# A factored one-hot for the first key, products four apart in PSUM, and another share of the activations per block

## The chip, the core and the metric

One core of a Trainium2 chip. TensorE does matmuls from SBUF into PSUM, VectorE the elementwise work, ScalarE activations and the reading out of PSUM, GpSimd issues the gathers, and a queue on SyncE issues the other transfers. The metric is the device time of one execution in microseconds, lower is better.

## What is computed

One layer of an encoder on 512 tokens of width 1024. The first half (sparse attention beside a pooling mixer) is not touched here. The second half looks up experts by product keys:

```python
def peer_ffn(h, w_q, sub_keys, u, v):          # by blocks of 128 tokens
    q = (hx @ w_q).reshape(TOKEN_BLOCK, PEER_HEADS, 2, PEER_HALF)
    s = jnp.einsum('nhpd,hpkd->nhpk', q, sub_keys)
    top_s, top_i = lax.top_k(s, PEER_TOPK)
    ...
    expert = (i1 * N_KEYS + i2).reshape(TOKEN_BLOCK, PEER_HEADS * PEER_TOPK)
    gate = jax.nn.softmax(best_s, axis=-1)
    act = jax.nn.gelu(jnp.einsum('nd,ned->ne', hx, u[expert]), approximate=False)
    return jnp.einsum('ne,ned->nd', gate * act, v[expert])
```

Each token takes 128 pairs (8 heads, 16 each) of a first key `i1` and a second key `i2`, both 0 to 127, with a gate each; there are 128 x 128 experts.

## The kernel before

Three of the four blocks of 128 tokens (384 tokens) are done densely: the activation of every expert is computed for all of them, times a table of gates that is zero where an expert wasn't chosen. The last block gathers its experts' rows.

The stage around the change I call the **gates stage**. Three kinds of work are recorded side by side there:

- The dense activations, `dense_acts`: 128 chunks of 128 experts. A chunk loads 512 KB of `uT`, ScalarE rounds it (`uhe`, line 517), VectorE makes the rest (`ule`, line 518), TensorE does 24 matmuls of 384 columns (`pse`, lines 554 to 556), ScalarE takes the gelu (line 563). 59 chunks are done in and around this stage, and the other 69 in the last stage, beside the contraction with `v`. `act_until(n)` records activations until n eighths of a chunk are there.
- The product keys of the coming block (`pk.pairs`, `pk.halves`): top 16 by VectorE, softmax, keys written to `sel`.
- The gates, `gates(tb)`, for blocks 0, 1 and 2. The keys and gates of a block are transposed, so that a partition is one of the 128 pairs and a column a token. Then for every 8 tokens VectorE makes two one-hot tables, `one` of the first key (line 614) and `two` of the second (line 615), each 128 x (8 tokens x 128 keys) in 16 bits, and multiplies `one` with the gates, which are in two 16-bit parts (line 620, twice). For each token TensorE multiplies `two` (as weights) with the gated `one`, one matmul of 128 columns per part, both into one 128 x 128 piece of PSUM (`gm`, line 626): the token's table of gates. Four tokens fill one PSUM tile; ScalarE scales it into `st` (line 627), where 16 tokens lie side by side per expert, so it writes single 4-byte values 64 bytes apart. Every 16 tokens a transfer of 1 MB writes `st` out to `gd`.

A step of 4 tokens is one `yield` of `gates`; after each step the loop records some of the keys' work and calls `act_until`, so that the activations are spread evenly over the 96 steps. The order of recording is not the whole order: the scheduler of the tile layer moves instructions of an engine past one another where their inputs and buffers allow. Each engine then runs its own list in that order. After the third block the chunks that are left run (`act_until` twice), and then the last stage opens, whose buffers take the place of this stage's.

Of the kernel before, what the change touches and what calls it, by code (L numbers as in the profile page):

```python
# [40 lines left out]
LEAD = 10  # L41
# [24 lines left out]
def layer(ctx, tc, xT, cvec, w_ada, cols, consts, w_in, w_grp, w_up, w_out, w_pq, subk, u, uT, v, out):  # L66
    nc = tc.nc
    V, A, T, G = nc.vector, nc.scalar, nc.tensor, nc.gpsimd
# [18 lines left out]
    iota = con[:, K_IOTA:K_IOTA + P]  # L87
    blk = con[:, K_BLK:K_BLK + P]

    with ExitStack() as pre:  # L90
# [110 lines left out]
        with ExitStack() as mix:  # L201
# [33 lines left out]
            with tc.tile_pool(name="xp", bufs=1, reuse_waits="tile") as xp, tc.tile_pool(name="xq", bufs=1, reuse_waits="tile") as xq, \  # L235
# [4 lines left out]
                ps = pst.tile([P, S], F32, name="n1s")  # L240
                part = tmp.tile([P, S], F32, tag="nf", name="n1p")
# [11 lines left out]
                for d in range(DT):  # L253
# [5 lines left out]
                    if rs is None:  # L259
# [3 lines left out]
                                           op0=ALU.add, op1=ALU.mult)  # L263
# [30 lines left out]
            ps = linear("q0", hh, hl)  # L294
# [41 lines left out]
            for i in range(4):  # L336
# [9 lines left out]
                ps = nxt  # L346
# [45 lines left out]
            for g in range(1, 4):  # L392
                ps = linear(f"p{g}", hh, hl)
# [5 lines left out]
            for j in range(DT):  # L399
                ps = linear(f"gp{j}", hh, hl)  # L400
# [130 lines left out]
    def multiply(w, n, name):  # L531
        return multiplies([w], n, [name])[0]
# [35 lines left out]
    with ExitStack() as win:  # L568
        kp = win.enter_context(tc.tile_pool(name="kp", bufs=1, reuse_waits="tile"))
        kt = win.enter_context(tc.tile_pool(name="kt", bufs=1, reuse_waits="tile"))  # L570
        oh = win.enter_context(tc.tile_pool(name="oh", bufs=2, reuse_waits="tile"))
        plg = win.enter_context(tc.tile_pool(name="plg2", bufs=2, space=PSUM, reuse_waits="tile"))
        pgm = win.enter_context(tc.tile_pool(name="pgm", bufs=2, space=PSUM, reuse_waits="tile"))
        ptr = win.enter_context(tc.tile_pool(name="ptr2", bufs=1, space=PSUM, reuse_waits="tile"))
        irep = kp.tile([P, NEXP, 2], F16, name="irep")
        V.tensor_copy(irep, iota.unsqueeze(2).to_broadcast([P, NEXP, 2]))
        pq = kp.tile([P, NH, S], F32, name="pq")
        sk = kp.tile([P, NH, P], F32, name="sk")
        nc.sync.dma_start(out=sk, in_=subk)
        pk = ProductKeys(nc, kp, kt, plg, pq, sk)  # L580
        for h in range(0, NH, 2):
            two = [fetch(w_pq[i], f"pq{i}") for i in (h, h + 1)]
            if h:
                two = [multiply(w, S, f"pq{h}_{i}") for i, w in enumerate(two)]
            else:
                two = multiplies(two, S, ["pq0_0", "pq0_1"])
            for i in range(2):
                A.copy(pq[:, h + i, :], two[i])
            for tb in range(2):
                pk.halves(tb, h)  # L590

        def gates(tb):

            tr = ptr.tile([P, 4, P], F32, tag="tr", name=f"gtr{tb}")
            for i, x in enumerate(sel[tb]):
                T.transpose(tr[:, i, :], x, ident)

            keys = oh.tile([P, 2, P], F16, tag="keys", name=f"keys{tb}", bufs=1)
            part = oh.tile([P, 2, P], F16, tag="part", name=f"part{tb}", bufs=1)
            gs = oh.tile([P, P], F32, tag="gs", name=f"gs{tb}", bufs=1)  # L600
            A.copy(keys, tr[:, 0:2, :])
            A.activation(gs, tr[:, 2, :], AF.Copy, scale=2.0 ** SCALED)
            A.copy(part[:, 0, :], gs)
            V.tensor_tensor(part[:, 1, :], gs, part[:, 0, :], op=ALU.subtract)

            full = [P, 4, NEXP, 2]
            pairs = lambda x, t: x[:, t:t + 8].rearrange("p (q j) -> p q j", j=2).unsqueeze(2).to_broadcast(full)
            numbers = irep.unsqueeze(1).to_broadcast(full)
            for g in range(P // GT):
                st = oh.tile([P, NEXP, GT], F32, tag="st", name=f"st{tb}_{g}", bufs=STB)  # L610
                for t8 in range(0, GT, 8):
                    t = g * GT + t8
                    one, two = [oh.tile(full, F16, tag=f"on{i}", name=f"on{i}_{tb}_{t}") for i in range(2)]
                    V.tensor_tensor(one, numbers, pairs(keys[:, 0, :], t), op=ALU.is_equal)  # L614
                    V.tensor_tensor(two, numbers, pairs(keys[:, 1, :], t), op=ALU.is_equal)  # L615
                    gated = []
                    for i in range(2):
                        x = oh.tile(full, F16, tag=f"oa{i}", name=f"oa{i}_{tb}_{t}")
                        gated.append(x)
                        V.tensor_tensor(x, one, pairs(part[:, i, :], t), op=ALU.mult)  # L620
                    for t4 in range(0, 8, 4):
                        ps = pgm.tile([P, 4, P], F32, tag="gm", name=f"gm{tb}_{t + t4}")
                        for k in range(4):
                            q, j = (t4 + k) // 2, k % 2
                            for i in range(2):
                                T.matmul(ps[:, k, :], two[:, q, :, j], gated[i][:, q, :, j], start=(i == 0), stop=(i == 1))  # L626
                        A.activation(st[:, :, t8 + t4:t8 + t4 + 4].rearrange("p e t -> p t e"), ps, AF.Copy, scale=2.0 ** -SCALED)  # L627
                        yield
                nc.sync.dma_start(out=gd[tb * (P // GT) + g], in_=st)

        sel = {}

        def select(tb):
            sel[tb] = [kt.tile([P, P], F32, tag=f"sel{i}", name=f"sel{tb}_{i}", bufs=2) for i in range(3)]
            return pk.pairs(tb, *sel[tb])

        def coming(tb):
            yield from select(tb)
            if tb + 1 < TB:
# [12 lines left out]
        for _ in select(0):
            act_until(done + DT)
        act_until(LEAD * DT)
        steps = P // 4
        between = (KEPT + SPILL - LEAD - TRAIL) * DT
        for tb in range(DENSE):
            keys = coming(tb + 1)
            for n, _ in enumerate(gates(tb)):
                if n * KEYS[tb] // steps != (n + 1) * KEYS[tb] // steps:  # L660
                    next(keys, None)
                act_until(LEAD * DT + between * (tb * steps + n + 1) // (DENSE * steps))
            for _ in keys:
                pass
        hs = kt.tile([P, DT, P], F32, tag="pr", name="hs")
        V.tensor_tensor(hs, h2h[:, :, ND:].bitcast(F32), h2l[:, :, ND:].bitcast(F32), op=ALU.add)
        for j0 in range(0, DT, 4):
            ps = ptr.tile([P, 4, P], F32, tag="tr", name=f"hxp{j0}")
            for j in range(4):
                T.transpose(ps[:, j, :], hs[:, j0 + j, :], ident)  # L670
            A.copy(hx[:, j0 * P:(j0 + 4) * P].rearrange("p (j t) -> p j t", t=P), ps)
        act_until((KEPT + SPILL) * DT)
        act_until(10 ** 6)
        k1, k2, g3 = sel[DENSE]
        V.scalar_tensor_tensor(e3, k1, 128.0, k2, op0=ALU.mult, op1=ALU.add)
        V.tensor_copy(gate3, g3)
# [80 lines left out]
    with tc.manual_schedule(engines={mybir.EngineType.DVE, mybir.EngineType.PE, mybir.EngineType.Activation}):  # L757
# [6 lines left out]
        for c in range(NEXP):  # L764
            a = c + KEPT
# [205 lines left out]
```

## Time and profile before

| | us |
|---|---|
| median of 3 runs (1596.89 to 1604.06) | 1600.07 |
| the profiled execution | 1600.14 |
| its span, first to last instruction | 1598.3 |
| gates stage, first gates' work on VectorE to the last gates' matmul | about 478 to 726 |
| its blocks | 478 to 563, 563 to 650, 650 to 726 |

The profile is read first by its 40 slices, then by windows of the one stage, by who waited for whom, by the chain of work that ended last, and by groups of instructions of one shape. A duration in a group is from an instruction's start to its end; neighbours on an engine can overlap by a little, so what one costs its engine is read from the starts of a row of them.

### The profile page before, as it was taken

Reading aid. Unit: us, or ns where it says so; the run is one execution under the profiler, and the core shown is the slowest. Engines: PE = TensorE matmul, PEld = TensorE weight load, DVE = VectorE, ACT = ScalarE, POOL = GpSimd, SP = SyncE. Lnnn points to the kernel's source line nnn. Section 1 sums busy time; section 2 is a strip of 40 time slices with the busy share of each in tenths; the row PEclk is TensorE's granted clock in tenths of the full one; section 3 lists DMA queues with packets and bytes.
Section 4 is the critical chain, followed back from the end, with each engine's and each line's share of the span. In section 5 each row is a group of like instructions: output and inputs, shape, how many; then the busy total and the mean of one; then the engine's idle time right before and its main releaser. Section 6 shows DMA issues by size and latency. Waiting matters only on the chain.

```text
span 1598.3 us, 22373 instructions
## 1 busy us (share of the span) xinstructions
PE 1540.0 (96%) x7977; PEld 1311.7 (82%) x7977; DVE 1311.6 (82%) x2658; ACT 691.3 (43%) x993; POOL 326.1 (20%) x318
## 2 busy tenths in 40 slices
PE   5999999999999999999999999999999999999998
PEld 3678766786789888899778999999999999987776
DVE  7799776658999999995668888888888888887777
ACT  4543445534446675674333333333333333333332
POOL 0000000000000000001113444444544445442320
PEclk9999999999999999999999999999999999999999
DMA  8412654333235454669889999999999999987874
GB/s 309 165 66 86 214 186 121 117 148 119 66 119 195 163 190 173 229 234 322 301 288 340 322 364 332 339 360 316 361 336 337 355 318 363 339 289 261 273 274 171
DMA packets 155105, 393.91 MB, mean 246 GB/s; under 512 B 13041, under 2 KB 67953, under 8 KB 151922
## 3 DMA queue, kind: packets, MB, share of 16 engines
q1 hardware_dynamic: 118130, 258.25, 46.5%
q0 software_dynamic: 36864, 134.23, 23.8%
q8 instruction: 62, 1.02, 0.3%
q14 instruction: 49, 0.40, 0.1%
HBM read 358.75 MB, written 33.69 MB: 246 GB/s over the span
## 4 chain that ended last, share of the span: by engine, by line
PE 48%; DVE 10%; DMA 5%; ACT 1%; issue 1%; SPq 0%; ACTq 0%; DVEq 0%
PE acc L748 28%; PE pse L540 6%; PE pse L539 6%; PE pse L538 6%; DMA v<-v 5%; DVE oa L620 2%; DVE ule L518 2%; DVE on L614 1%; DVE on L615 1%; ACT vh L738 1%; DVE vl L740 1%; PE pse L556 1%; PE pse L555 1%; PE pse L554 1%; PE gm L626 0%
## 5 line engine op out<-in xcount | busy, mean ns | idle before, releaser
L689 POOL DMA_INDIRECT ur<-u,ei x128 | 158.0, 1234 | 638.7 <-ACT Wh L737 395.0
L748 PE MATMUL acc<-vh,Wh 128*128 128x512 f32 x768 | 240.3, 394 | 14.6 <-ACT vh L738 14.6
L748 PE MATMUL acc<-vl,Wh 128*128 128x512 f32 x768 | 241.2, 395 | 2.0 <-DVE vl L740 1.9
L748 PE MATMUL acc<-vh,Wl 128*128 128x512 f32 x768 | 240.1, 394 | 0.0
L740 DVE TENSOR_TENSOR vl<-v,vh 128x1024 fp32r<-128x1024 f32 x128 | 156.9, 1226 | 83.0 <-ACT vh L738 70.7
L697 POOL DMA_INDIRECT vr<-v,ei x128 | 165.2, 1291 | 232.7 <-DVE sacc L702 204.2
L540 PE MATMUL pse<-h2h,ule 128*128 128x384 f32 x552 | 185.1, 335 | 0.0
L539 PE MATMUL pse<-h2l,uhe 128*128 128x384 f32 x552 | 184.6, 334 | 0.0
L538 PE MATMUL pse<-h2h,uhe 128*128 128x384 f32 x552 | 184.4, 334 | 0.0
L737 ACT ACTIVATE Wh<-gelu 128x384 fp32r<-128x384 f32 x106 | 55.6, 525 | 290.1 <-PE acc L748 187.5
L748 PEld LDWEIGHTS acc<-vh,Wh 128*128 128x128 f32 x768 | 144.7, 190 | 41.6 <-ACT vh L738 16.7
L748 PEld LDWEIGHTS acc<-vl,Wh 128*128 128x128 f32 x768 | 145.7, 191 | 35.3 <-DVE vl L740 5.3
L748 PEld LDWEIGHTS acc<-vh,Wl 128*128 128x128 f32 x768 | 146.2, 190 | 30.9
L518 DVE TENSOR_TENSOR ule<-ue,uhe 128x1024 fp32r<-128x1024 f32 x128 | 155.9, 1218 | 19.0 <-ACT uhe L517 19.0
L554 PE MATMUL pse<-h2h,uhe 128*128 128x384 f32 x472 | 166.2, 352 | 1.0 <-ACT gelu L563 1.0
L556 PE MATMUL pse<-h2h,ule 128*128 128x384 f32 x472 | 161.1, 342 | 4.7 <-DVE ule L518 4.5
L702 DVE SCALAR_TENSOR_TENSOR sacc<-vr,wt,sacc 128x1024 f32<-128x1024 f32 x127 | 162.8, 1282 | 2.4
L555 PE MATMUL pse<-h2l,uhe 128*128 128x384 f32 x472 | 159.6, 338 | 0.0
L517 ACT ACTIVATE uhe<-ue 128x1024 fp32r<-128x1024 f32 x128 | 134.8, 1053 | 53.8 <-PE pse L555 36.0
L691 DVE SCALAR_TENSOR_TENSOR ur<-ur,hx 128x1024 f32<-128x1024 f32 x128 | 150.7, 1220 | 1.5 <-DMA ur<-u,ei 1.5
L738 ACT ACTIVATE vh<-v 128x1024 fp32r<-128x1024 f32 x128 | 135.7, 1060 | 36.0 <-DMA v<-v 35.7
L627 ACT ACTIVATE st<-gm 128x512 f32<-128x512 f32 x96 | 101.2, 1092 | 53.9 <-PE gm L626 49.6
(412 smaller groups left out, 2757.3 us busy)
## 6 DMA issues: line engine op xcount, KB each, us to landing
ue<-uT SPq DMA_DIRECT2D x128, 512.0 KB
v<-v SPq DMA_DIRECT2D x128, 512.0 KB
wada<-w_ada SPq DMA_DIRECT2D x48, 512.0 KB
gd<-st SPq DMA_DIRECT2D x24, 1024.0 KB
g<-gd SPq DMA_DIRECT2D x16, 1536.0 KB
ad<-gelu SPq DMA_DIRECT2D x22, 192.0 KB
wgp<-w_in SPq DMA_DIRECT2D x8, 512.0 KB
wga<-w_in SPq DMA_DIRECT2D x8, 512.0 KB
```

The costliest lines, as they stand in the source:

```text
L518: V.tensor_tensor(lo, src, hi.bitcast(F32), op=ALU.subtract)
L538: T.matmul(p, hi[:, k, :], h2h[:, k, :n], start=(k == 0), stop=False)
L539: T.matmul(p, hi[:, k, :], h2l[:, k, :n], start=False, stop=False)
L540: T.matmul(p, lo[:, k, :], h2h[:, k, :n], start=False, stop=(k == DT - 1))
L554: T.matmul(ps, hi[:, k, :], h2h[:, k, :ND], start=(k == 0), stop=False)
L555: T.matmul(ps, hi[:, k, :], h2l[:, k, :ND], start=False, stop=False)
L556: T.matmul(ps, lo[:, k, :], h2h[:, k, :ND], start=False, stop=(k == DT - 1))
L689: G.indirect_dma_start(out=ur, out_offset=None, in_=u, in_offset=bass.IndirectOffsetOnAxis(ap=ei3[:, k:k + 1], axis=0))
L697: G.indirect_dma_start(out=vr, out_offset=None, in_=v, in_offset=bass.IndirectOffsetOnAxis(ap=ei3[:, k:k + 1], axis=0))
L702: V.scalar_tensor_tensor(sacc, vr, wt[:, k:k + 1], sacc, op0=ALU.mult, op1=ALU.add)
L740: V.tensor_tensor(vl, vr, vh.bitcast(F32), op=ALU.subtract)
L748: T.matmul(acc[tb][i], x[:, t], y[:, i * 512:(i + 1) * 512], start=(c == 0 and n == 0), stop=(c == NEXP - 1 and n == 2))
```

## The change

The first key is split as 16 a + b, with a from 0 to 7 and b from 0 to 15. `low` is b, `keys[:, 0, :]` becomes 16 a (four small instructions a block). For every 32 tokens VectorE makes `rest`, the one-hot of b over 16 numbers (128 x 512), `ten`, the one-hot of a over 8 (128 x 256), and `gt`, `ten` times each part of the gates (twice 128 x 256). The gated table of 8 tokens is then a product of `gt` and `rest`, spread over 8 x 16 keys (128 x 1024, twice as before); `one` is gone.

The order of the axes in the gated table, in the PSUM tile and in the reading out is another: the PSUM tile is `[128, 128 keys, 4 tokens]`, so a matmul writes its 128 columns 16 bytes apart, and ScalarE reads the tile straight through and writes four tokens (16 bytes) at a time, 64 bytes apart.

`FILL` sets the share of the activations that is recorded by the end of each block: 0.36, 0.72 and 1.0, in place of a third each.

```diff
+tens = kp.tile([P, NEXP // KL, 8], F16, name="tens")
+V.tensor_copy(tens, iota.rearrange("p (a b) -> p a b", b=KL)[:, :, 0:1].to_broadcast([P, NEXP // KL, 8]))
...
+ki = oh.tile([P, P], I32, tag="ki", name=f"ki{tb}", bufs=1)
+V.tensor_copy(ki, keys[:, 0, :])
+V.tensor_scalar(ki, ki, KL - 1, None, op0=ALU.bitwise_and)
+V.tensor_copy(low, ki)
+V.tensor_tensor(keys[:, 0, :], keys[:, 0, :], low, op=ALU.subtract)
...
+                if g * GT % TG == 0:
+                    rest = oh.tile([P, TG // 2, KL, 2], F16, tag="rest", name=f"rest{tb}_{g}")
+                    V.tensor_tensor(rest, numbers(TG // 2, KL), pairs(low, t, TG).to_broadcast([P, TG // 2, KL, 2]), op=ALU.is_equal)
+                    ten = oh.tile([P, NG, NA, 8], F16, tag="ten", name=f"ten{tb}_{g}")
+                    V.tensor_tensor(ten, tens.unsqueeze(1).to_broadcast([P, NG, NA, 8]), eights(keys[:, 0, :], t), op=ALU.is_equal)
+                    for i in range(2):
+                        V.tensor_tensor(gt[i], ten, eights(part[:, i, :], t), op=ALU.mult)
...
-                    V.tensor_tensor(one, numbers, pairs(keys[:, 0, :], t), op=ALU.is_equal)
...
-                        V.tensor_tensor(x, one, pairs(part[:, i, :], t), op=ALU.mult)
+                        V.tensor_tensor(x, gt[i][:, n].rearrange("p a (q j) -> p a q j", j=2).unsqueeze(3).to_broadcast([P, NA, 4, KL, 2]),
+                                        rest[:, 4 * n:4 * n + 4].unsqueeze(1).to_broadcast([P, NA, 4, KL, 2]), op=ALU.mult)
...
-                        ps = pgm.tile([P, 4, P], F32, tag="gm", name=f"gm{tb}_{t + t4}")
+                        ps = pgm.tile([P, P, 4], F32, tag="gm", name=f"gm{tb}_{t + t4}")
...
-                                T.matmul(ps[:, k, :], two[:, q, :, j], gated[i][:, q, :, j], start=(i == 0), stop=(i == 1))
-                        A.activation(st[:, :, t8 + t4:t8 + t4 + 4].rearrange("p e t -> p t e"), ps, AF.Copy, scale=2.0 ** -SCALED)
+                                T.matmul(ps[:, :, k], two[:, q, :, j], gated[i][:, :, q, :, j], start=(i == 0), stop=(i == 1))
+                        A.activation(st[:, :, t8 + t4:t8 + t4 + 4], ps, AF.Copy, scale=2.0 ** -SCALED)
...
-                act_until(LEAD * DT + between * (tb * steps + n + 1) // (DENSE * steps))
+                f0, f1 = (FILL[tb - 1] if tb else 0.0), FILL[tb]
+                act_until(LEAD * DT + int(between * (f0 + (f1 - f0) * (n + 1) / steps)))
```

VectorE at the start of the first block, before (`on` is a one-hot table, `oa` a gated one, `ule` an activation chunk's; the numbers are block and first token):

```order
L614 TENSOR_TENSOR on_0_0_4072<-irep,keys_4064 128x1024
L604 TENSOR_TENSOR part_4065<-gs_4066,part_4065 128x128
L615 TENSOR_TENSOR on_0_0_4073<-irep,keys_4064 128x1024
L620 TENSOR_TENSOR oa_0_0_4076<-on_0_0_4072,part_4065 128x1024
L620 TENSOR_TENSOR oa_0_0_4078<-on_0_0_4072,part_4065 128x1024
L614 TENSOR_TENSOR on_0_8_4128<-irep,keys_4064 128x1024
L615 TENSOR_TENSOR on_0_8_4129<-irep,keys_4064 128x1024
L620 TENSOR_TENSOR oa_0_8_4132<-on_0_8_4128,part_4065 128x1024
L620 TENSOR_TENSOR oa_0_8_4134<-on_0_8_4128,part_4065 128x1024
L518 TENSOR_TENSOR ule_4166<-ue_4164,uhe_4165 128x1024
```

and now (lines are those of the changed file; `ki` and `low` split the key):

```order
L613 CAST ki_4074<-keys_4066 128x128
L639 TENSOR_TENSOR on_0_0_4088<-irep,keys_4066 128x1024
L610 TENSOR_TENSOR part_4068<-gs_4069,part_4068 128x128
L614 TENSOR_SCALAR ki_4074<-ki_4074 128x128
L639 TENSOR_TENSOR on_0_8_4142<-irep,keys_4066 128x1024
L615 CAST low_4067<-ki_4074 128x128
L877 TENSOR_TENSOR sel_0_4158<-pr_4620 128x128
L616 TENSOR_TENSOR keys_4066<-keys_4066,low_4067 128x128
L628 TENSOR_TENSOR rest_0_4080<-irep,low_4067 128x512
L630 TENSOR_TENSOR ten_0_4082<-tens,keys_4066 128x256
L521 TENSOR_TENSOR ule_4178<-ue_4176,uhe_4177 128x1024
L634 TENSOR_TENSOR gt_0_0_4084<-ten_0_4082,part_4068 128x256
```

The gated table of the first 8 tokens stood right behind its two one-hot tables; now the four that split the key (`ki`, `low`, `keys`) and the small tables (`rest`, `ten`, `gt`) stand ahead of it.

VectorE a little later in the same block, before, for the third and fourth 8 tokens:

```order
L614 TENSOR_TENSOR on_0_16_4201<-irep,keys_4064 128x1024
L615 TENSOR_TENSOR on_0_16_4202<-irep,keys_4064 128x1024
L620 TENSOR_TENSOR oa_0_16_4205<-on_0_16_4201,part_4065 128x1024
L620 TENSOR_TENSOR oa_0_16_4207<-on_0_16_4201,part_4065 128x1024
L614 TENSOR_TENSOR on_0_24_4271<-irep,keys_4064 128x1024
L518 TENSOR_TENSOR ule_4229<-ue_4227,uhe_4228 128x1024
L615 TENSOR_TENSOR on_0_24_4272<-irep,keys_4064 128x1024
L620 TENSOR_TENSOR oa_0_24_4275<-on_0_24_4271,part_4065 128x1024
L620 TENSOR_TENSOR oa_0_24_4277<-on_0_24_4271,part_4065 128x1024
```

and now:

```order
L628 TENSOR_TENSOR rest_2_4355<-irep,low_4067 128x512
L639 TENSOR_TENSOR on_0_16_4216<-irep,keys_4066 128x1024
L645 TENSOR_TENSOR oa_0_16_4218<-gt_0_0_4084,rest_0_4080 128x1024
L645 TENSOR_TENSOR oa_0_16_4220<-gt_0_0_4086,rest_0_4080 128x1024
L521 TENSOR_TENSOR ule_4239<-ue_4237,uhe_4238 128x1024
L639 TENSOR_TENSOR on_0_24_4287<-irep,keys_4066 128x1024
L645 TENSOR_TENSOR oa_0_24_4289<-gt_0_0_4084,rest_0_4080 128x1024
L645 TENSOR_TENSOR oa_0_24_4291<-gt_0_0_4086,rest_0_4080 128x1024
```

Of the four wide instructions of 8 tokens three are left; `rest` of the next 32 tokens stands among them.

TensorE where the third block's first gates' matmul stands (the number behind `pse` is the chunk of the activations), before:

```order
L556 MATMUL pse39_6445<-h2h_2650,ule39_6356 128x384
L554 MATMUL pse39_6445<-h2h_2650,uhe39_6355 128x384
L555 MATMUL pse39_6445<-h2l_2651,uhe39_6355 128x384
L626 LDWEIGHTS on1_2_0_6400
L626 MATMUL gm2_0_6407<-oa0_2_0_6403,on1_2_0_6400 128x128
```

and now:

```order
L559 MATMUL pse42_6599<-h2h_2650,ule42_6525 128x384
L557 MATMUL pse42_6599<-h2h_2650,uhe42_6524 128x384
L558 MATMUL pse42_6599<-h2l_2651,uhe42_6524 128x384
L652 LDWEIGHTS on1_2_0_6501
L652 MATMUL gm2_0_6507<-oa0_2_0_6503,on1_2_0_6501 128x128
```

The third block begins within chunk 42 in place of chunk 39. Counted in matmuls of `pse` over the whole list, the first gates' matmul of the blocks stands behind 11.2, 25.0 and 39.7 chunks before and behind 11.8, 26.4 and 42.2 now; the last one of the third block stands behind 52.5 in both.

## Rows read from the trace of the kernel before

**Rows 1.** The page of the profile: the span, and the span in 40 slices of 40 us (busy tenths).

```profile
span 1598.3 us, 22373 instructions
...
PE   5999999999999999999999999999999999999998
...
DVE  7799776658999999995668888888888888887777
```

**Rows 2.** Busy time by stretch, for the three blocks of the gates stage and for the whole of it: start and end, length, then the busy us (and instructions) of each engine, the granted clock, the DMA share and GB/s.

```profile
478.00:563.00 85.00, 79.82 (x619) 73.00 (x620) 83.22 (x230) 55.32 (x72) 0.00 (x0) 1.00 0.52 189
563.00:650.00 87.00, 82.85 (x613) 74.12 (x611) 86.70 (x291) 55.54 (x72) 0.00 (x0) 1.00 0.50 174
650.00:726.00 76.00, 75.50 (x598) 70.03 (x598) 75.11 (x181) 55.70 (x64) 0.00 (x0) 1.00 0.68 242
478.00:726.00 248.00, 238.18 (x1826) 217.15 (x1827) 245.02 (x700) 166.56 (x207) 0.00 (x0) 1.00 0.56 200
```

**Rows 3.** Who waited for whom in the gates stage (478 to 726 us): total us, times, longest us.

```profile
ACT st L627 <- PE gm L626: 49.6, 49, 2.5
...
PE gm L626 <- DVE oa L620: 5.7, 8, 1.8
...
DVE ule L518 <- ACT uhe L517: 1.5, 5, 0.4
...
DVE on L614 <- ACT keys L601: 0.7, 1, 0.7
...
DVE top L835 <- ACT kss L832: 0.5, 2, 0.3
```

**Rows 4.** The chain that ended last, pieces of 672 to 800 us in order of time (start us, us, what): the third block, its end, and what follows it.

```profile
672.70 1.21 DVE oa L620 x2
673.91 0.60 DVE on L614
674.51 0.60 DVE on L615
675.11 1.14 DVE ule L518
...
726.05 1.24 DVE hs L666
...
739.92 6.53 DMA v<-v
```

**Rows 5.** VectorE between 440 and 730 us by line and shape: count, busy us in total, mean ns of one, idle time before them.

```profile
L620 DVE TENSOR_TENSOR oa<-on,part 128x1024 f16<-128x1024 f16 x96 | 62.6, 684 | 0.0
L518 DVE TENSOR_TENSOR ule<-ue,uhe 128x1024 fp32r<-128x1024 f32 x51 | 62.0, 1216 | 3.0 <-ACT uhe L517 3.0
...
L614 DVE TENSOR_TENSOR on<-irep,keys 128x1024 f16<-128x1024 f16 x48 | 32.5, 682 | 0.7 <-ACT keys L601 0.7
...
L850 DVE TENSOR_TENSOR pr<-pr 128x256 bf16<-128x256 bf16 x12 | 3.4, 285 | 0.0
...
L889 DVE CAST at<-pos 128x128 bf16<-128x128 uint32 x4 | 1.0, 261 | 0.0
...
L902 DVE TENSOR_TENSOR off<-at,off 128x128 bf16<-128x128 bf16 x4 | 0.9, 214 | 0.0
...
L850 DVE TENSOR_TENSOR pr<-k_1h 128x512 bf16<-128x512 bf16 x2 | 0.8, 416 | 0.0
```

**Rows 6.** VectorE in order of time, in the second block (start us, us, engine, line, operation): how closely one follows the next.

```profile
571.22 0.69 DVE L614 TENSOR_TENSOR on<-irep,keys 128x1024 f16<-128x1024 f16 x1
571.83 0.68 DVE L615 TENSOR_TENSOR on<-irep,keys 128x1024 f16<-128x1024 f16 x1
572.43 1.28 DVE L620 TENSOR_TENSOR oa<-on,part 128x1024 f16<-128x1024 f16 x2
```

**Rows 7.** TensorE in the gates stage by line and shape.

```profile
L554 PE MATMUL pse<-h2h,uhe 128*128 128x384 f32 x333 | 118.6, 356 | 1.0 <-ACT gelu L563 1.0
L556 PE MATMUL pse<-h2h,ule 128*128 128x384 f32 x333 | 113.4, 341 | 1.2 <-DVE ule L518 1.2
L555 PE MATMUL pse<-h2l,uhe 128*128 128x384 f32 x334 | 112.8, 338 | 0.0
L626 PE MATMUL gm<-oa,on 128*128 128x128 f16 x768 | 62.5, 220 | 6.4 <-DVE oa L620 5.7 <-ACT st L627 0.6
L829 PE MATMUL ks<-sk,pq 64*128 64x128 f32 x52 | 7.8, 301 | 1.4 <-ACT kss L832 1.2
```

**Rows 8.** TensorE in order of time, in the first block: the starts of the activations' matmuls, and a bundle of 14 matmuls of the gates between two of them.

```profile
485.10 0.33 PE L555 MATMUL pse<-h2l,uhe 128*128 128x384 f32 x1
485.27 0.33 PE L556 MATMUL pse<-h2h,ule 128*128 128x384 f32 x1
...
487.10 0.98 PE L626 MATMUL gm<-oa,on 128*128 128x128 f16 x14
487.88 0.42 PE L556 MATMUL pse<-h2h,ule 128*128 128x384 f32 x1
```

**Rows 9.** ScalarE between 380 and 730 us by line and shape.

```profile
L627 ACT ACTIVATE st<-gm 128x512 f32<-128x512 f32 x96 | 101.2, 1092 | 53.9 <-PE gm L626 49.6 <-issue 2.5 <-ACT gelu L563 1.0
...
L588 ACT COPY pq<-pspq 128x512 f32<-128x512 f32 x6 | 3.4, 572 | 0.0
```

**Rows 10.** The stretch just after the gates stage, by windows (columns as in rows 2).

```profile
726.00:760.00 34.00, 33.56 (x188) 32.08 (x187) 14.22 (x18) 13.66 (x20) 5.05 (x5) 1.00 1.00 335
```

More of the change, by code (lines that the diff above doesn't have):

```diff
@@ L48 @@
 UPS = 2
+KL = 16
+TG = 32
+FILL = (0.36, 0.72, 1.0)
 SCALED = 14
@@ L598, in gates @@
             keys = oh.tile([P, 2, P], F16, tag="keys", name=f"keys{tb}", bufs=1)
+            low = oh.tile([P, P], F16, tag="low", name=f"low{tb}", bufs=1)
             part = oh.tile([P, 2, P], F16, tag="part", name=f"part{tb}", bufs=1)
@@ L604, in gates @@
             V.tensor_tensor(part[:, 1, :], gs, part[:, 0, :], op=ALU.subtract)
-            full = [P, 4, NEXP, 2]
-            pairs = lambda x, t: x[:, t:t + 8].rearrange("p (q j) -> p q j", j=2).unsqueeze(2).to_broadcast(full)
-            numbers = irep.unsqueeze(1).to_broadcast(full)
+            ki = oh.tile([P, P], I32, tag="ki", name=f"ki{tb}", bufs=1)
+            V.tensor_copy(ki, keys[:, 0, :])
+            V.tensor_scalar(ki, ki, KL - 1, None, op0=ALU.bitwise_and)
+            V.tensor_copy(low, ki)
@@ L609, in gates @@
+            V.tensor_tensor(keys[:, 0, :], keys[:, 0, :], low, op=ALU.subtract)
+            NA, NG = NEXP // KL, TG // 8
+            pairs = lambda x, t, n: x[:, t:t + n].rearrange("p (q j) -> p q j", j=2).unsqueeze(2)
+            numbers = lambda q, n: irep[:, :n, :].unsqueeze(1).to_broadcast([P, q, n, 2])
+            eights = lambda x, t: x[:, t:t + TG].rearrange("p (g x) -> p g x", x=8).unsqueeze(2).to_broadcast([P, NG, NA, 8])
             for g in range(P // GT):
                 st = oh.tile([P, NEXP, GT], F32, tag="st", name=f"st{tb}_{g}", bufs=STB)
+                if g * GT % TG == 0:
+                    t = g * GT
+                    rest = oh.tile([P, TG // 2, KL, 2], F16, tag="rest", name=f"rest{tb}_{g}")
+                    V.tensor_tensor(rest, numbers(TG // 2, KL), pairs(low, t, TG).to_broadcast([P, TG // 2, KL, 2]), op=ALU.is_equal)
+                    ten = oh.tile([P, NG, NA, 8], F16, tag="ten", name=f"ten{tb}_{g}")
+                    V.tensor_tensor(ten, tens.unsqueeze(1).to_broadcast([P, NG, NA, 8]), eights(keys[:, 0, :], t), op=ALU.is_equal)
+                    gt = []
+                    for i in range(2):
+                        gt.append(oh.tile([P, NG, NA, 8], F16, tag=f"gt{i}", name=f"gt{i}_{tb}_{g}"))
+                        V.tensor_tensor(gt[i], ten, eights(part[:, i, :], t), op=ALU.mult)
@@ L611, in gates @@
                 for t8 in range(0, GT, 8):
                     t = g * GT + t8
-                    one, two = [oh.tile(full, F16, tag=f"on{i}", name=f"on{i}_{tb}_{t}") for i in range(2)]
-                    V.tensor_tensor(one, numbers, pairs(keys[:, 0, :], t), op=ALU.is_equal)
-                    V.tensor_tensor(two, numbers, pairs(keys[:, 1, :], t), op=ALU.is_equal)
+                    full = [P, 4, NEXP, 2]
+                    two = oh.tile(full, F16, tag="on1", name=f"on1_{tb}_{t}")
+                    V.tensor_tensor(two, numbers(4, NEXP), pairs(keys[:, 1, :], t, 8).to_broadcast(full), op=ALU.is_equal)
@@ L616, in gates @@
                     gated = []
+                    n = t % TG // 8
                     for i in range(2):
-                        x = oh.tile(full, F16, tag=f"oa{i}", name=f"oa{i}_{tb}_{t}")
+                        x = oh.tile([P, NA, 4, KL, 2], F16, tag=f"oa{i}", name=f"oa{i}_{tb}_{t}")
                         gated.append(x)
-                        V.tensor_tensor(x, one, pairs(part[:, i, :], t), op=ALU.mult)
+                        V.tensor_tensor(x, gt[i][:, n].rearrange("p a (q j) -> p a q j", j=2).unsqueeze(3).to_broadcast([P, NA, 4, KL, 2]),
+                                        rest[:, 4 * n:4 * n + 4].unsqueeze(1).to_broadcast([P, NA, 4, KL, 2]), op=ALU.mult)
```

## Prediction, made before the changed kernel ran

> **What bounds the kernel now.** The slices come first: TensorE shows nines nearly throughout, but VectorE shows an unbroken run of them only from the 11th to the 18th slice, 400 to 720 us, where keys and gates are made [rows 1]. So the stage of the change is taken by itself, by windows. [...] TensorE's busy time overstates it, since its matmuls overlap: the matmuls of the activations last 338 to 356 ns [rows 7] but start 0.17 to 0.18 us apart, and 14 matmuls of the gates take 0.78 us, 0.056 us each [rows 8]. What it needs is therefore some 1000 x 0.174 = 174 us for the activations (333 + 333 + 334 of them) [rows 7], 768 x 0.056 = 43 us for the gates, and about 6 for the keys (52 that last 0.30 us and overlap): 223 of 248 us. The waits say the same: VectorE waits 1.5 + 0.7 + 0.5 us, for ScalarE, TensorE's gates wait for VectorE 5.7 us, and ScalarE waits for TensorE 49.6 us [rows 3]. The chain from 672 us to the first work behind the stage, at 726, is VectorE's, one instruction at the end of the other [rows 4]. **VectorE sets this stage's length, and TensorE stands 25 us behind it.** Both figures matter: a saving on VectorE pays only until TensorE is reached.
>
> **The change part by part.** All times are made against the profiled execution, 1600.14 us with a span of 1598.3; the median is 1600.07, so a difference applies to it unchanged.
>
> *What VectorE loses.* The 48 instructions of `one` [rows 5]. Each lasts 0.68 us, but the next one starts 0.60 us after it [rows 4, 6], so 48 x 0.60 = 29 us.
>
> *What it gets.* Per 32 tokens one 128 x 512 and three 128 x 256 in 16 bits. The rows of that size are 416 and 285 ns [rows 5]; with the overlap of 0.08 us between neighbours [rows 6] they take 0.34 and 0.20, without it (where one needs the result just ahead, as `gt` needs `ten`) the full time. That is 0.94 to 1.27 us, times 12: 11 to 15 us. Splitting the key is four instructions of 128 x 128 a block; the nearest rows are a cast of 261 ns and a subtraction of 214 ns [rows 5], so 0.65 to 1.0 us a block, 2 to 3 us in all. The two gated products stay at 128 x 1024, and I take them at the present 0.60 us; they read runs of two values from `gt`, as they now read runs of two from `part`. `tens` is made once, ahead of the stage, for 0.2 us. Together 13 to 18 us; **VectorE saves 11 to 16 us, and I take 13**: 232 us are left.
>
> *Moved activations.* A chunk brings VectorE 1.14 us (`ule` in the chain) [rows 4] and TensorE 24 x 0.174 = 4.2 us. By the counts in the order the third block has 10.3 chunks in place of 12.8, the first two 30.4 in place of 28.5, and 0.6 lie ahead of the stage. The sums by block, gates' matmuls 14.3 us each: in the third, VectorE 75.1 - 4.3 - 2.9 = 68 us against TensorE's 10.3 x 4.2 + 14 = 58; in the first two together, VectorE 83.2 + 86.7 - 8.7 + 2.2 = 163 us against TensorE's 30.4 x 4.2 + 29 + 6 = 163 (2.2 for the 1.9 chunks). So the two engines come out level there, and VectorE alone decides in the third block. The stage is then 231 to 232 us, plus the 3 us in which VectorE isn't busy now, plus what two level engines lose in waiting for each other. For that no row stands ready: it is between nothing and the 5.7 us that TensorE's gates wait now [rows 3]; I take 3. Stage: 238 us, **10 us shorter**.
>
> *Reading out of PSUM.* ScalarE's instruction lasts 1092 ns where it writes values 64 bytes apart, and 572 ns for the same 512 values written side by side [rows 9]. Writing 16 bytes at a time lies between; up to 96 x 0.52 = 50 us of ScalarE go. None of it is on the path: ScalarE waits for TensorE half as long, and VectorE waits for it 2.7 us in the stage [rows 3]. Cost and gain nil. The cover is VectorE's length; ScalarE would have to grow by 81 us to come through it.
>
> *Writing products 16 bytes apart in PSUM.* No row of this trace has a matmul that writes with gaps. The bounds: nothing, since the same matmul already reads its moving operand with gaps (every second 16-bit value) at 0.056 us per 128 columns, 0.44 ns a column, against 0.174/384 = 0.45 ns for matmuls that read side by side [rows 8]; at the other end the 1.0 ns a value that gaps cost ScalarE on the write side [rows 9], 0.13 us a matmul, 100 us in all. A gain is excluded, since the rate without gaps is already that of the other matmuls. I take nothing, the row of the same instruction on the same engine, and make the rest a rival.
>
> *After the stage.* From 726 us TensorE does the chunks left over and VectorE idles (14.2 of 34 us) while transfers run at a share of 1.00 [rows 10]; the first load of `v` in the chain comes at 740 [rows 4]. All of that follows the end of the gates, so it moves up as a whole. The stage's own transfers use a share of 0.56 [rows 2]; the same bytes in 238 us make 0.58.
>
> Sum: 1600.1 - 10 = **1590 us**, with 1584 to 1596 as its own range (VectorE saving 16 with no loss; 11 with a loss of 7).
>
> **The rivals.** *First, gaps in PSUM slow the gates' matmuls, and the kernel becomes slower.* The place is line 626; the matmul would become TensorE's bound. If it slows by the factor that gaps cost ScalarE, 1092/572 = 1.9 [rows 9], the 43 us become 82, TensorE needs 262 us, and with 3 us of losses the stage is 265 in place of 248: 1617 us. It decides from 25 us on (0.033 us a matmul), where TensorE's 223 reach the present 248; from 10 us on it begins to eat the gain. For it: a write with gaps costs the one engine here that makes one almost double. Against: that engine writes to SBUF, and the reads with gaps on TensorE cost nothing [rows 8]. The far end, 100 us, would give 1678.
>
> [...]
>
> *Second, the gain is lost on the way.* In the first two blocks the engines are level (163 us each), so any delay counts: a smaller slowing of the matmuls (0.01 to 0.03 us each, 8 to 23 us, in place of headroom), or the longer start of a block, where TensorE's first gates now wait for a string of dependent small instructions. It would leave 0 to 5 us of the 10: 1595 to 1603, middle 1599. For it: TensorE's first gates of a block wait already; against: VectorE stays busy with them, and they are in the sum.
>
> *Third, the change doesn't do what it says:* the gated product, whose two inputs are both spread, falls to the rate of the 32-bit instructions, 1216 against 684 ns [rows 5]. 96 x 0.53 = 51 us more on VectorE: 232 + 51 + 3 = 286, 1638 us. Against: the product of before has a spread input too.
>
> **How the numbers follow.** Forecast 0.52; slower by the writes 0.25; lost on the way 0.20; third rival 0.03. What a measurement here can tell from no change is about 0.5%, 8 us, so faster means below 1592, slower above 1608. Of the forecast's 0.52, 0.38 lies below 1592 and 0.14 within the bound. Lost on the way lies within it but for 0.02 below. Of the writes' 0.25, 0.03 lie within the bound, at a small factor. So faster 0.40, same 0.35, slower 0.25. For 8 times in 10 the range needs the forecast, the second rival and half of the first: 1584 to 1618. The likeliest case's own range stands above.
>
> **What would show it.** VectorE: no 128 x 1024 instructions on the line of `one`, 12 of 128 x 512 at some 0.41 us and 36 of 128 x 256 at some 0.28, the 96 gated products still at 0.68 us (third rival: 1.2). ScalarE: the reading out at 0.6 us rather than 1.09. TensorE: bundles of gates' matmuls still 0.056 us apart; 0.08 or more is the first rival. The stage: 238 us with VectorE still the one that is never idle; if TensorE is the one, and VectorE waits more than 10 us, it is the first or the second rival. The chain of the first two blocks should begin to hold stretches of TensorE. Behind the stage the length to the end should stay at 872 us (1598 less 726); a longer one would mean that the transfers and not the gates set where the last stage starts, and would make the sum wrong too.

## The result, and the profile after

The changed kernel takes 1622.08 us (median of 4, 1619.53 to 1626.42) against 1598.94 us before (median of 4): a ratio of 1.0143, 95% interval 1.0108 to 1.0177. It is slower by 23 us. The forecast was 1590 us with a range to 1618; the first rival was 1617 us.

The gates stage by windows, with the columns of [rows 2]. The blocks now end at about 567, 664 and 746 us:

```profile
478.00:567.00 89.00, 87.18 (x598) 81.20 (x596) 72.54 (x208) 38.62 (x64) 0.00 (x0) 1.00 0.49 167
567.00:664.00 97.00, 96.86 (x659) 90.13 (x658) 88.92 (x312) 47.01 (x78) 0.00 (x0) 1.00 0.48 175
664.00:746.00 82.00, 81.12 (x562) 75.93 (x559) 71.30 (x191) 39.83 (x64) 0.00 (x0) 1.00 0.60 214
478.00:746.00 268.00, 265.16 (x1813) 247.26 (x1811) 232.76 (x709) 125.46 (x205) 0.00 (x0) 1.00 0.52 184
```

The stage takes 268 us in place of 248. VectorE, busy 245.0 of 248 us before, is busy 232.8 of 268; ScalarE fell from 166.6 to 125.5. TensorE went up, from 238.2 of 248 to 265.2 of 268. Its rows, as in [rows 7], and a bundle of 8 matmuls of the gates in order of time, as in [rows 8]:

```profile
L557 PE MATMUL pse<-h2h,uhe 128*128 128x384 f32 x329 | 118.3, 359 | 0.0
...
L652 PE MATMUL gm<-oa,on 128*128 128x128 f16 x768 | 101.0, 307 | 2.8 <-DVE oa L645 2.7
L856 PE MATMUL ks<-sk,pq 64*128 64x128 f32 x52 | 5.0, 297 | 0.0
```

```profile
487.72 0.33 PE L559 MATMUL pse<-h2h,ule 128*128 128x384 f32 x1
487.90 1.05 PE L652 MATMUL gm<-oa,on 128*128 128x128 f16 x8
488.70 0.42 PE L557 MATMUL pse<-h2h,uhe 128*128 128x384 f32 x1
488.96 0.34 PE L558 MATMUL pse<-h2l,uhe 128*128 128x384 f32 x1
```

The bundle of 8 takes 0.80 us to the start of the next matmul; 14 took 0.78 us before [rows 8]. The chain that ended last, pieces in the third block (start us, us, what), has what each costs on the path:

```profile
693.04 0.89 PE gm L652 x8
694.63 0.18 PE pse L558
694.99 0.18 PE pse L557
695.52 0.89 PE gm L652 x8
```

Eight matmuls take 0.89 us of the chain, 0.111 us each. Side by side, eight take 0.47 us of a chain (first experiment, below), 0.059 us each. The 0.056 of the prediction was counted from start to start, where eight now take 0.80 us, 0.100 each; the two ways of counting are kept apart below. The chain was VectorE's [rows 4]; it is TensorE's now. By these prices TensorE needs 987 x 0.174 = 172 us for the activations, 768 x 0.111 = 85 for the gates and 5 for the keys: 262 of 268 us.

Who waits, with the columns of [rows 3]:

```profile
ACT st L653 <- PE gm L652: 99.2, 69, 2.8
...
DVE ule L521 <- ACT uhe L520: 14.0, 13, 3.0
...
DVE on L639 <- PE gm L652: 7.9, 12, 1.5
...
DVE oa L645 <- PE gm L652: 5.4, 6, 1.8
DVE top L862 <- ACT kss L859: 5.0, 6, 1.4
...
PE gm L652 <- DVE oa L645: 2.7, 2, 1.8
```

VectorE waits 32 us where it waited 2.7, on TensorE's gates directly (`on`, `oa`: the tables' buffers) and on the rounding of the activations. ScalarE waits 99 us for products in place of 50. VectorE's and ScalarE's instructions last as the prediction had it (columns as in [rows 5, 9]):

```profile
L645 DVE TENSOR_TENSOR oa<-gt,rest 128x1024 f16<-128x1024 f16 x96 | 62.5, 684 | 5.4 <-PE gm L652 5.4
...
L634 DVE TENSOR_TENSOR gt<-ten,part 128x256 f16<-128x256 f16 x24 | 5.9, 283 | 0.0
L628 DVE TENSOR_TENSOR rest<-irep,low 128x512 f16<-128x512 f16 x12 | 5.0, 415 | 0.0
...
L630 DVE TENSOR_TENSOR ten<-tens,keys 128x256 f16<-128x256 f16 x12 | 3.4, 283 | 0.0
```

```profile
L653 ACT ACTIVATE st<-gm 128x512 f32<-128x512 f32 x96 | 57.4, 598 | 107.4 <-PE gm L652 99.2 <-issue 7.3
```

The wide product kept its 684 ns, the small tables cost 415 and 283 ns, and reading out fell from 1092 to 598 ns. From the start of the last product to the end of the span the profiled execution takes 5 us longer than before (1624.7 - 745.4 = 879 us against 1598.3 - 724.5 = 874). The code there is the same, and two profiled executions of one and the same kernel (the one with pairs, below) differ there by 8 us (1586.5 - 714.0 = 872 and 1599.1 - 718.5 = 881), so nothing is read from it.

### The profile page after: what moved, and what is told of

The parts are those of the page before. It is cut to its first block, busy times and chain, and to the rows that moved or that the text cites. A ratio compares the mean times of both kernels' runs of the same rounds, so it can differ in the third digit from the quotient of the medians.

```text
span 1624.7 us, 22381 instructions
## 1 busy us (share of the span) xinstructions
PE 1571.9 (97%) x7977; PEld 1345.3 (83%) x7977; DVE 1299.1 (80%) x2671; ACT 650.6 (40%) x993; POOL 324.2 (20%) x318
## 4 chain that ended last, share of the span: by engine, by line
PE 83%; DVE 8%; DMA 6%; ACT 2%; issue 1%; SPq 0%; ACTq 0%; DVEq 0%
PE acc L775 26%; PE pse L543 6%; PE pse L542 6%; PE pse L541 6%; DMA v<-v 5%; PE gm L652 5%; PE pse L557 4%; PE pse L559 4%; PE pse L558 4%; PE po L454 1%; PE psga L172 1%; PE psga L170 1%; PE psga L171 1%; PE pso L170 1%; PE psgp L170 1%; PE psgp L172 1%
## 5 line engine op out<-in xcount | busy, mean ns | idle before, releaser
L542 PEld LDWEIGHTS pse<-h2l,uhe 128*128 128x128 f32 x552 | 103.6, 188 | 3.2
## 6 DMA issues: line engine op xcount, KB each, us to landing
g<-gd SPq DMA_DIRECT2D x16, 1536.0 KB, 14.5
```

What stands on the lines that cost most here:

```text
L542: T.matmul(p, hi[:, k, :], h2l[:, k, :n], start=False, stop=False)
```

## The experiments

**Products side by side again**, all else as in the changed kernel.

```diff
-ps = pgm.tile([P, P, 4], F32, ...)
+ps = pgm.tile([P, 4, P], F32, ...)
-T.matmul(ps[:, :, k], two[:, q, :, j], gated[i][:, :, q, :, j], ...)
+T.matmul(ps[:, k, :], two[:, q, :, j], gated[i][:, :, q, :, j], ...)
-A.activation(st[:, :, t8 + t4:t8 + t4 + 4], ps, ...)
+A.activation(st[:, :, t8 + t4:t8 + t4 + 4].rearrange("p e t -> p t e"), ps, ...)
```

> The changed kernel, but the four products of a PSUM tile lie side by side again and ScalarE writes single values 64 bytes apart, as before; the factored one-hot and the new shares of activations stay. Theory W (a matmul that writes its columns with gaps in PSUM takes twice as long): the gates' matmuls are 0.056 us apart again, VectorE sets the stage's length, the stage takes some 238 us and the kernel 1590 us (1584 to 1596). Theory R (the matmul is slower because its moving operand is now read in 8 runs of 16): they stay 0.10 us apart, TensorE sets the length, 1620 us. Theory L (it is the one-hot's small instructions or the moved activations that cost the time): 0.056 us apart, but over 1605 us.

Measured: 1595.69 us, ratio to the kernel before 0.9963 (0.9945 to 0.9981). A bundle of 8 matmuls on TensorE, and the stage by windows:

```profile
488.55 0.63 PE L652 MATMUL gm<-oa,on 128*128 128x128 f16 x8
488.99 0.42 PE L557 MATMUL pse<-h2h,uhe 128*128 128x384 f32 x1
489.24 0.34 PE L558 MATMUL pse<-h2l,uhe 128*128 128x384 f32 x1
```

```profile
478.00:722.00 244.00, 234.88 (x1824) 216.40 (x1823) 231.57 (x712) 165.99 (x206) 0.00 (x0) 0.99 0.58 203
```

Eight take 0.44 us to the next start again, with the moving operand read in the new order. That is W's price; R is out, and L too. In both layouts the activations' first matmul behind a bundle is followed after 0.25 to 0.26 us (488.70 to 488.96, 488.99 to 489.24), where the step elsewhere is 0.174. With that step counted in, eight matmuls cost TensorE 488.96 - 487.90 - 0.174 = 0.89 us with gaps and 489.24 - 488.55 - 0.174 = 0.52 us without: 0.37 us for eight, and for all 768 some 36 us.

The gain is 4 us in the stage, though, where 10 were forecast: VectorE is busy 231.6 us, as forecast (232), but it is idle for 12 of the 244, where the forecast had 6 (3 as before, and 3 for the waits of two level engines). Its waits there:

```profile
DVE ule L521 <- ACT uhe L520: 7.1, 7, 2.2
DVE top L862 <- ACT kss L859: 3.6, 7, 0.8
```

W also had VectorE set the stage's length, and that is not so. The chain of the stage by line, and two pieces of the third block:

```profile
by line: PE pse L557 22.1%; PE pse L559 20.7%; PE pse L558 20.1%; PE gm L652 16.9%; DVE ule L521 3.2%; ACT st L653 2.4%; PE ks L856 1.6%; DVE oa L645 1.5%; DVE on L639 1.0%; issue 0.9%; DVE kss L864 0.9%; DVE tix L863 0.9%; DVE tix L866 0.8
...
671.86 0.47 PE gm L652 x8
672.33 0.23 PE pse L557
```

80% of the chain (the first four entries) is TensorE's activations and gates. By the prices above TensorE needs about 996 x 0.174 + 96 x 0.52 + 5 = 228 us here (an estimate), beside VectorE's 231.6: taken over the whole stage the two engines are level, and a wait on either side counts.

**Products four apart alone**, in the kernel before.

```diff
-ps = pgm.tile([P, 4, P], F32, ...)
+ps = pgm.tile([P, P, 4], F32, ...)
-T.matmul(ps[:, k, :], two[:, q, :, j], gated[i][:, q, :, j], ...)
+T.matmul(ps[:, :, k], two[:, q, :, j], gated[i][:, q, :, j], ...)
-A.activation(st[:, :, t8 + t4:t8 + t4 + 4].rearrange("p e t -> p t e"), ps, ...)
+A.activation(st[:, :, t8 + t4:t8 + t4 + 4], ps, ...)
```

> The kernel before with nothing changed but the products four apart in PSUM and ScalarE's reading that goes with it. W: matmuls of the gates 0.104 us apart; TensorE then needs 223 + 768 x 0.048 = 260 us of a stage in which VectorE needs 245, so the stage grows by 12 to 20 us: 1612 to 1620 us. R or L: the matmuls stay at 0.056 us, ScalarE's reading is shorter, 1598 to 1600 us.

Measured: 1624.83 us, 1.0143 (1.0107 to 1.0179). TensorE's gates and the stage:

```profile
L626 PE MATMUL gm<-oa,on 128*128 128x128 f16 x768 | 101.7, 306 | 2.6 <-DVE oa L620 2.5
```

```profile
478.00:751.00 273.00, 269.07 (x1823) 249.56 (x1824) 249.03 (x702) 127.08 (x206) 0.00 (x0) 1.00 0.52 183
```

This one part makes the whole loss, and about 5 us more than W gave (1612 to 1620 us, with a stage of 260 to 268; the stage is 273 us): 306 ns a matmul as in the changed kernel, with the one-hot, the moving operand and the shares of before.

**Products two apart**: a column every 8 bytes.

```diff
-ps = pgm.tile([P, P, 4], F32, ...)
+ps = pgm.tile([P, 2, P, 2], F32, ...)
-T.matmul(ps[:, :, k], ...)
+T.matmul(ps[:, k // 2, :, k % 2], ...)
-A.activation(st[:, :, t8 + t4:t8 + t4 + 4], ps, ...)
+A.activation(st[:, :, t8 + t4:t8 + t4 + 4].rearrange("p e (h j) -> p e h j", j=2), ps.rearrange("p h e j -> p e h j"), ...)
```

> The changed kernel with products two apart in PSUM: a matmul writes its columns 8 bytes apart in place of 16. If any gap costs the full price (W, one value of a pair at a time): 0.10 us apart, 1620 us, as the changed kernel. If the price grows with the distance: some 0.08 us apart, TensorE needs 241 us, level with VectorE, 1595 to 1608 us. R: 0.10 us and 1620 us as well, so this run tells the two forms of W apart only with the first run.

Measured: 1623.66 us, 1.0134 (1.0105 to 1.0163). The bundle of 8:

```profile
488.07 1.05 PE L652 MATMUL gm<-oa,on 128*128 128x128 f16 x8
488.88 0.42 PE L557 MATMUL pse<-h2h,uhe 128*128 128x384 f32 x1
```

0.81 us to the next start, against 0.80 at 16 bytes: the full price at half the distance. Between 8 and 16 bytes it doesn't grow.

**Pairs of keys side by side**: two columns together, then 24 bytes of gap.

```diff
-ps = pgm.tile([P, P, 4], F32, ...)
+ps = pgm.tile([P, P // 2, 4, 2], F32, ...)
-T.matmul(ps[:, :, k], ...)
+T.matmul(ps[:, :, k, :], ...)
-A.activation(st[:, :, t8 + t4:t8 + t4 + 4], ps, ...)
+A.activation(st[:, :, t8 + t4:t8 + t4 + 4].rearrange("p (a b) k -> p a b k", b=2), ps.rearrange("p a k b -> p a b k"), ...)
```

> The changed kernel with pairs of keys kept together in PSUM: the tile is [64 pairs of keys, 4 tokens, 2 keys], so a matmul writes two columns side by side, then a gap of 24 bytes; ScalarE reads single values 8 bytes apart (its order is key, token) and writes four tokens side by side as in the changed kernel. If the price of a gap is paid per pair of values (one access for two values side by side): gates' matmuls 0.056 us apart, the stage as with products side by side (244 us) or shorter, 1588 to 1596 us. If any break of the run costs the full price: 0.10 us apart and 1622 us. In between (some 0.08 us): 1600 to 1610.

Measured: 1590.16 us, 0.9945 (0.9920 to 0.9970). The bundle, ScalarE's reading, the stage, and VectorE's waits:

```profile
490.75 0.63 PE L652 MATMUL gm<-oa,on 128*128 128x128 f16 x8
491.19 0.42 PE L557 MATMUL pse<-h2h,uhe 128*128 128x384 f32 x1
```

```profile
L653 ACT ACTIVATE st<-gm 128x512 f32<-128x512 f32 x96 | 56.7, 597 | 73.8 <-PE gm L652 66.6 <-issue 3.5 <-ACT st L653 3.1
```

```profile
478.00:715.00 237.00, 230.45 (x1810) 212.51 (x1810) 228.88 (x706) 124.23 (x205) 0.00 (x0) 1.00 0.59 207
```

```profile
DVE ule L521 <- ACT uhe L520: 4.6, 4, 2.2
DVE top L862 <- ACT kss L859: 1.8, 3, 0.7
```

0.44 us for 8, against 0.80 and 0.81 with single values: the price is paid for a value that stands alone, not for a gap. (Each pair starts at a multiple of 8 bytes of the tile; pairs that start 4 bytes later were not run.) ScalarE reads single values 8 bytes apart and still takes 597 ns. The stage is 237 us, with VectorE busy 229, and its two longest waits fell from 7.1 and 3.6 us in the first experiment to 4.6 and 1.8 (4.6 and 2.6 in the second measurement). A second measurement of the same kernel, beside the last two experiments below:

> The kernel with pairs of keys side by side in PSUM once more, with more rounds, to have its gain with a narrower interval beside the two runs below: 1588 to 1593 us, 0.5 to 0.8% below the kernel before.

Measured: 1593.79 us, 0.9946 (0.9930 to 0.9962): the ratio as expected, the time 0.8 us above the range. It is faster than both the kernel before and the changed one. Of the kernels tried that compute everything it has the lowest ratio, but it can't be told from those at 0.9956 to 0.9963, whose intervals overlap with its own. The stage in its profiled execution:

```profile
478.00:719.00 241.00, 234.72 (x1826) 216.64 (x1825) 232.23 (x717) 125.16 (x207) 0.00 (x0) 0.99 0.59 206
```

That is 241 us where the first profiled execution of the same kernel had 237, so differences of 4 us between the stages of single executions, here and below, show nothing by themselves.

**Products side by side, read with gaps**: matmuls as in the first experiment, ScalarE reads four tokens 512 bytes apart and writes them side by side.

```diff
-A.activation(st[:, :, t8 + t4:t8 + t4 + 4].rearrange("p e t -> p t e"), ps, ...)
+A.activation(st[:, :, t8 + t4:t8 + t4 + 4], ps.rearrange("p t e -> p e t"), ...)
```

> Products side by side as in the first experiment, but ScalarE reads them with gaps (four tokens 512 bytes apart in PSUM) and writes four tokens side by side. It asks where ScalarE's 1092 ns come from, and whether its queue is what VectorE waits for. If the write with gaps is what costs: some 0.6 us an instruction, else 1.0 or more. Theory S (VectorE's waits for the rounding of the activations come from ScalarE's queue, full of readings of 1.09 us): they go, the stage is 236 to 238 us, 1588 to 1591 us. Theory C (they come from TensorE, which has not released the buffer of two chunks back): the waits stay, the stage is within 2 us of 244, 1593 to 1597 us.

Measured: 1594.92 us, 0.9956 (0.9938 to 0.9974).

```profile
L653 ACT ACTIVATE st<-gm 128x512 f32<-128x512 f32 x96 | 56.7, 597 | 74.8 <-PE gm L652 67.6 <-issue 3.5 <-ACT st L653 3.1
```

```profile
478.00:717.00 239.00, 232.49 (x1813) 214.38 (x1812) 229.43 (x707) 124.39 (x205) 0.00 (x0) 0.99 0.59 205
```

It is ScalarE's write that costs: 597 ns with the reads far apart, against 1089 ns in the first experiment, which reads straight through and writes 64 bytes apart. The stage is 239 us, 5 shorter than with the long reading, and VectorE is idle for 10 us rather than 12. That lies between S's range (236 to 238) and C's (242 to 246). The wait that S names fell from 7.1 to 5.1 us and did not go:

```profile
DVE ule L521 <- ACT uhe L520: 5.1, 5, 2.2
```

The total, 1594.92, lies in C's range and can't be told from the first experiment's (0.9963). The run doesn't settle between S and C.

**Three buffers** for the two halves of an activation chunk, products side by side.

```diff
-hi = up.tile([P, DT, P], F32R, tag="uh", name=f"uh{name}")
-lo = up.tile([P, DT, P], F32R, tag="ul", name=f"ul{name}")
+hi = up.tile([P, DT, P], F32R, tag="uh", name=f"uh{name}", bufs=3)
+lo = up.tile([P, DT, P], F32R, tag="ul", name=f"ul{name}", bufs=3)
-HOLD = 38
-SPILL = 22
+HOLD = 33
+SPILL = 27
```

> Products side by side, and three buffers in place of two for the two halves of an activation chunk (uh, ul); to make room 33 activation tiles are held in place of 38 and 27 spilled in place of 22. C: VectorE waits less than 4 us for the rounding (12 to 16 with two buffers), the stage is 235 to 240 us. S, or if VectorE's lost time is something else: no change in the stage, 244 us. The total also carries the five more spilled tiles, 2 MB of 394, which I put at 0 to 3 us: C 1587 to 1593 us.

Measured: 1594.95 us, 0.9962 (0.9941 to 0.9983), as the first experiment.

```profile
478.00:720.00 242.00, 233.98 (x1816) 215.75 (x1815) 228.72 (x711) 165.66 (x206) 0.00 (x0) 0.98 0.59 206
```

```profile
DVE ule L521 <- ACT uhe L520: 7.1, 6, 2.2
```

VectorE waits the same 7.1 us for the rounding and is idle for 13 of 242 us. C falls in the form in which it was put: a third buffer doesn't bring the lost time back. The rounding itself still waits 14.5 us for TensorE's activations, in place of 16.1 in the first experiment.

**Half the products**, products side by side.

```diff
-for i in range(2):
-    T.matmul(ps[:, k, :], two[...], gated[i][...], start=(i == 0), stop=(i == 1))
+T.matmul(ps[:, k, :], two[...], gated[0][...], start=True, stop=True)
```

> Products side by side, with only the first of the two matmuls per token (the second part of the gates is left out of the product; VectorE still makes it). TensorE has 384 x 0.056 = 21 us less to do, VectorE the same. C (the gain of the one-hot is lost because TensorE, with two buffers, is often the later one): VectorE's idle time falls from 12 to 3 or 4 us, stage 235 to 237 us, 1587 to 1590 us. If VectorE's idle time has another cause: stage 243 to 244 us, 1594 to 1597 us.

Measured: 1590.95 us, 0.9948 (0.9923 to 0.9973).

```profile
478.00:706.00 228.00, 214.92 (x1433) 194.94 (x1433) 220.65 (x689) 163.79 (x205) 0.00 (x0) 0.99 0.63 217
```

The total lies in neither range. The stage shrank to 228 us, below both expectations, and VectorE is idle for 7 of them: some of VectorE's work also left the stage (busy 220.7 us in place of 231.6), so the run doesn't separate what it was made to separate. It shows something else. 16 us less stage than the first experiment's gave 5 us in the total. The chain behind the stage:

```profile
735.10 10.64 DMA v<-v
...
768.82 10.39 DMA v<-v
...
804.39 12.47 DMA v<-v
```

Three loads of `v` of 10 to 12 us stand in it, from 735 us on; the first experiment's chain has two such loads up to 825 us, of 10.6 and 11.8 us. One load more, and the 11 us of VectorE's work that has to be done later, could each account for what was lost; no run shows which it was.

**Equal thirds, and the short reading alone.** Two more, to price the parts: the kernel with pairs with the activations in equal thirds, and the kernel before with nothing but ScalarE's reading with gaps (the same line as above).

```diff
-FILL = (0.36, 0.72, 1.0)
+FILL = (1 / 3, 2 / 3, 1.0)
```

> The same with the activations in equal thirds: what the new shares bring by themselves. If the third block is where TensorE and VectorE are level without them (chunks 12.8 in place of 10.3, 53 + 14 us of matmuls against 71 us of VectorE), they bring little, 0 to 2 us. If they bring what the first and the fourth experiment differed by, 3 to 4 us: 1593 to 1596.

Measured: 1594.12 us, 0.9956 (0.9940 to 0.9972); beside 0.9946 (0.9930 to 0.9962) with the new shares (the second measurement of the pairs), so their part can't be told from nothing.

> The kernel before with nothing changed but the way ScalarE reads: products side by side, read with gaps of 512 bytes, four tokens written side by side (0.6 us in place of 1.09). With the one-hot not factored VectorE is busy 245 of 248 us, so a shorter reading should bring nothing: 1598 to 1601 us (the prediction's view, cost and gain nil). If ScalarE's queue delays VectorE also here: 1595 us or less.

Measured: 1599.40 us, 0.9990 (0.9974 to 1.0006): no difference. The stage by windows:

```profile
478.00:726.00 248.00, 240.45 (x1835) 219.47 (x1836) 245.80 (x702) 125.47 (x207) 0.00 (x0) 0.99 0.57 201
```

ScalarE is down to 125 us, and VectorE is busy 245.8 of 248 as before: nothing to gain.

**The one-hot alone**, the first experiment with equal thirds.

> The factored one-hot alone: products side by side, activations in equal thirds. W: VectorE saves 11 to 16 us; against the first run only the shares differ, and since VectorE sets the length in all three blocks, they should matter little: 1588 to 1596 us, within 4 us of the first run. R and L: 1605 us and more.

Measured: 1599.43 us, 0.9986 (0.9974 to 0.9999); the stage is the first experiment's:

```profile
478.00:722.00 244.00, 233.89 (x1819) 214.80 (x1818) 230.99 (x713) 166.06 (x206) 0.00 (x0) 1.00 0.58 203
```

W's range was missed: 2 us of gain in place of 4 to 12, with VectorE busy 231 of 244 us. It is 3.7 us slower than the first experiment, though the stages of the two profiled executions are equally long; the intervals of the two ratios overlap (0.9974 to 0.9999, 0.9945 to 0.9981).

## Why the prediction was wrong

*What bounds the kernel:* right, but TensorE stood nearer than it said. VectorE, busy 245 of 248 us [rows 2], set the length. TensorE's 223 leaves out the longer step behind each bundle. Before, next to [rows 8]:

```profile
488.14 0.33 PE L554 MATMUL pse<-h2h,uhe 128*128 128x384 f32 x1
```

The 14 matmuls cost 488.14 - 487.10 - 0.174 = 0.87 us, 0.062 each, and eight side by side 0.52 us, 0.065 each (first experiment). So the gates need some 48 to 50 us in place of 43, TensorE some 229 (an estimate), and the point from which the sign turns was nearer 19 us of TensorE than 25.

*What VectorE saves:* right. 13 us were taken; it is busy 231.6 us in the first experiment, 13.4 less than before. The wide product kept its rate, so the third rival is out.

*Writing products 16 bytes apart:* this is the step that failed: "I take nothing, the row of the same instruction on the same engine". That row showed the matmul *reading* with gaps, and it was set above the one row in the trace of an engine *writing* with gaps, ScalarE's factor of 1.9. On TensorE's chain the factor is 0.89/0.47 = 1.9, and in all the gaps cost some 36 us, more than TensorE stood behind. The first two experiments show that it is the write and nothing else (0.44 us for eight side by side with the operand in its new order; 306 ns a matmul with gaps and the operand of before, against 220 [rows 7]), the third that 8 bytes cost what 16 do (0.81 and 0.80 us for eight), and the pairs that two neighbours in each run are enough to escape it (0.44 us). Why a value that stands alone costs more, no run shows. The rival had the mechanism, the place, TensorE's 262 us and all but 3 us of the stage. That 262 is partly luck: it started from 223, some 6 us too low, and added 39 for gaps that cost 36. The range ended inside the rival because I had given it a quarter and taken half of that.

*Reading out of PSUM, "cost and gain nil":* right for the kernel before, where the short reading alone gives 0.9990 (0.9974 to 1.0006). Once VectorE has less to do it is open. With equal thirds, the short reading and pairs together take the factored one-hot from 0.9986 (0.9974 to 0.9999) to 0.9956 (0.9940 to 0.9972), some 5 us. With the new shares the short reading alone takes it from 0.9963 to 0.9956, which is within the noise.

*What two level engines lose, 3 us:* too small. VectorE is idle for 12 to 13 of 242 to 244 us with the long reading and for 8 to 10 with the short one, of which 3 were there before. The prediction had the engines level in the first two blocks and VectorE alone deciding in the third. The first experiment has TensorE in 80% of the stage's chain, in the third block too, and the pairs' first profiled execution 81%; the 6 us that TensorE's 223 left out are part of this. Which wait costs how much stays open; a third activation buffer doesn't change it. So even without the gaps the forecast's 1590 would have come out as 1595.69; with the short reading and pairs it is 1590.16 and 1593.79. The first experiment lies where the second rival had it (1595 to 1603, for two level engines). Of that rival's two causes the slower matmuls are out (0.055 us apart), and the longer start of a block shows: from a block's last product to the next one's first go 8 and 10 us on TensorE, where 4 and 3 went before. TensorE does activations meanwhile, and its gates' idle waits for VectorE stay at 5.8 us (5.7 before), so what this cost isn't shown.

*Moved activations:* they were given no price of their own, and with the pairs they have none that shows. With products side by side and the long reading they go with 3.7 us (0.9986 and 0.9963), at intervals that overlap.

## What to carry to other kernels

Before a tile's axes are turned for its reader's sake, price the writer: here eight of TensorE's products took 0.44 us with two fp32 columns side by side in PSUM, as with all 128, and 0.80 with single ones, and the reader could take the gaps, for ScalarE's reading took 597 ns with single values 8 or 512 bytes apart and 598 straight through. Where no row shows an access, take the price from the row with the same direction (write for write; a factor of 1.9 on both engines here), even if it is another engine's, and when it turns the sign let the range reach past it. A saving on the bound engine is paid out only up to the next engine: 13 us on VectorE gave 2 us alone and some 6 with the new shares, with TensorE then level, and 7 to 9 with a shorter ScalarE instruction and pairs. And when a bundle of matmuls is priced, count to the second start behind it: the step that follows is part of the price (here 0.25 to 0.26 us in place of 0.174).

## What was not expected of the hardware

- A matmul of 128 columns that writes single fp32 values 16 bytes apart takes 0.111 us of TensorE's chain, against 0.059 side by side. From start to start 8 of them take 0.80 us at 16 bytes, 0.81 at 8 bytes, and 0.44 both side by side and with two values together and 24 bytes of gap. The granted clock of these stages was 0.99 or 1.00.
- Behind a bundle of such matmuls the step between the first two of the activations is 0.25 to 0.26 us in place of 0.174, with gaps in the products or without.
- ScalarE's 512 values from PSUM take 1092 ns written 64 bytes apart (1086 to 1089 in the first and the last experiment) and 596 to 598 ns written in runs of 16 bytes, read straight through or 8 or 512 bytes apart.
